# An fp32 mLSTM/attention backbone: activation table loaded during the first transfers, two sums placed later, and key casts regrouped ahead of a layer norm

## The chip, the cores and the metric

The kernel runs on one core of a Trainium2 chip. The metric is the device time of one execution in microseconds (us). The kernel before took 1350.44 us (median of 3 runs, 1350.17 to 1350.73).

## The reference

A backbone of two layers (`DEPTH = 2`) over 256 latent tokens and 256 context tokens of width 1024. Layer 0 mixes tokens with a bidirectional chunkwise mLSTM, layer 1 with multi-head latent attention with a low-rank key/value path; behind each mixer stands a gated convolutional FFN. Each sub-layer reads a modulated input and ends in a layer norm:

```python
# per sub-layer, shift/scale/gate from SiLU(c) @ w_ada + b
h = x * (1 + scale) + shift
x = layer_norm(ALPHA * x + gate * sublayer(h))

# latent attention, layer 1 (cut): kv is compressed, normed, and expanded per head
ckv = rms_norm(h @ w_dkv[..., :256]);  kr = rope(h @ w_dkv[..., 256:])
k_nope = ckv @ w_uk      # 8 heads x 128
v      = ckv @ w_uv      # 8 heads x 128
```

The context stream goes through the same weights with its own modulation and reads only context; the latent stream reads both.

## The kernel before

**Numbers.** Every fp32 operand is split in two parts: a rounded high part (`hi`, a cast on ScalarE, ACT) and the remainder (`lo`, a subtraction on VectorE, DVE). A product is three matmuls on TensorE (PE): hi·hi, hi·lo, lo·hi. `mm3` issues them at L427, L430 and L431, so these three lines hold most matmul rows of the profile, and the names in a row (`y<-w,fz`, `kn<-ckT,wu`, `dkv<-w,hl`) tell which product it is. For activations, `split` issues the cast (L441) and the subtraction (L442).

**Weights** come in banks through a class `Stream`. `_split` casts the high part of a bank on ACT (L344), `low` subtracts its low part on DVE (L367). Low parts of the second pair of `dkv` banks (the layer-1 compression) are kept back and issued by `release`. `pump` runs a stream ahead. `behind(i, others)` fixes that an instruction is queued after others of its own engine; it adds no wait between engines.

**Start.** `start_up` writes the first 20 us out by hand for PE, DVE and ACT: the DMA order in `LOADS`, the instruction order in `STEPS`. `WARM` idle matmuls (L651, product of zeros) come first. Then, by the step letters: `Q` SiLU of the conditioning vector on ACT (L656, `cond`); `a0`/`b0` the two halves of the first 128-wide modulation product (L506, `adar<-adaw,cond`); `I3` three idle matmuls (L667); `C0` copies the product out (ACT); `T0`/`O0` transpose it and make columns; `e0` modulates the first input tile; `w0`, `y0` cast the first weights; `P00`.. are the up-projection matmuls (L714). Every DMA of this stretch is queued on SyncE (SP) at L636.

**Between the layers.** `w_fout0` computes the FFN-out of layer 0 by a Strassen-like scheme: seven products are accumulated in PSUM banks and combined with each other by DVE in the steps of a generator (`sums`); at L1735 the banks of the last product `p7` get the partial sums `u2` added, two instructions of 512 columns. In the same stretch DVE makes the low parts of the weight banks `y21`, `y22` and of `fz`, which PE reads next. 

Then come two layer norms: of the context (a step list `mid(0, ...)`) and of the latent tokens (`mid(1, ...)`), each two row tiles. `z_norm` handles a row tile with `mv` and `rs` (statistics), the first 512 columns on DVE (L1812) and the other 512 on ACT (L1814). `ln_T` transposes the result (16 PE transposes, L1278), applies the norm's scale and shift on ACT (L1284) and DVE (L1285), and splits it into `hc` or `hl`, the input of `dkv`. In its context form `ln_T` calls `release` at its steps 2 and 4. The latent norm is not run as one block: `tick` advances it by a step at points of `build`'s tail, among `mla_kv` (RMS norm and transposes of the compressed kv, `ckr`, `ckT`), `ukn` (keys of eight heads, two heads of 256 columns to a PSUM bank) and `uv` (values). ACT, DVE and PE run their queues strictly in program order.

Of the kernel before, what the change touches and what calls it, by code (L numbers as in the profile page):

```python
# [10 lines left out]
AF = mybir.ActivationFunctionType  # L11
ALU = mybir.AluOpType
# [15 lines left out]
H1 = 8  # L28
# [24 lines left out]

NUP = 5
GATES = 11
WARM = 10
LOADS = (
    "a00 c a01 w0 x0 a10 a11 w1 x1 a20 a21 w2 x2 a30 a31 w3 x3 a40 a41 w4 x4 a50 a51 w5 x5 a60 a61 w6 x6 "
    "a70 a71 x7 w7 s u0 g0").split()
STEPS = (  # L60
# [3 lines left out]
    "A7 C7 K7 V53 T7 O7 V60 E7 k7 V61 H7 V62 V63 V70 V71 V72 V73 U0 V24 V34 V44 V54 V64 V74 M0").split()  # L64
# [81 lines left out]
def _pack(i):  # L146
# [8 lines left out]
    uqr = np.ascontiguousarray(uq[:, :, DN:]).reshape(384, H1 * DR)  # L155
    qn_blocks = np.concatenate([_stat(uqn, h, 0, 3) for h in range(H1)], axis=1)
    kn_blocks = np.concatenate([_stat(ukn, h, 0, 2) for h in range(H1)], axis=1)
    dkv_s = (0, 3, 6)
    for key, (n, cols) in ids.items():
# [97 lines left out]
class Stream:  # L257
# [107 lines left out]
    def low(self, j, src, h, l):  # L365
        n = src.shape[1]
        i = self.k.nc.vector.tensor_sub(l[:, :n], src, h[:, :n])  # L367
        self.k.behind(i, self.behind)
        self.made = i
        self.raw.pop(j)  # L370
        while self._room():
            self._load()
        return i
# [24 lines left out]
class K:  # L398
# [203 lines left out]
    def start_up(self):  # L602

        nc, st = self.nc, self.st
# [9 lines left out]
        for step in LOADS:  # L614
            op, n = step[0], [int(x) for x in step[1:]]
            if op == "a":
                t = raw[step] = self.uf("adaw")
                src = self.a["ada0"][2 * n[0] + n[1]]
            elif op == "x":
                t = raw[step] = self.s2("xT")  # L620
                src = self.a["tokT"][n[0]]
            elif op == "w":
                t = raw[step] = self.pool.tile([128, CW], F32, tag=tag[n[0]][0], name="raw0", bufs=tag[n[0]][1])
                c = slice(0, nw if n[0] < 2 else 512)
                t, src = t[:, c], self.a["up0"][n[0]][:, c]
            elif op == "u":
                t = raw[step] = self.pool.tile([128, CW], F32, tag="raw", name="up4", bufs=NRAW)
                t, src = t[:, :768], self.a["up4"]
            elif op == "c":
                t, src = self.sm0, self.a["sm0"]  # L630
            elif op == "g":
                t = self.gw = self.pool.tile([128, 16, 32], F32, tag="s2", name="gw", bufs=NS)
                src = self.a["gw"]
            else:
                t, src = self.sm, self.a["sm"]
            i = nc.sync.dma_start(t, src)  # L636
# [5 lines left out]
        w = {k: (t[:, 0], t[:, 1]) for k, t in zip((3, 4, 5), w3)}  # L642
        w[0] = [self.pool.tile([128, CW], F32R, tag="acc", name="w0", bufs=2) for _ in range(2)]

        e = mybir.EngineType
        idle = self.ps("idle")
        rows, adas, hT = {}, {}, {}
        ps, made = {}, [0] * NUP
        with self.tc.manual_schedule(engines={e.PE, e.DVE, e.Activation}):
            for _ in range(WARM):  # L650
                nc.tensor.matmul(idle, self.zero[:, 0:128], self.zero, start=True, stop=True)  # L651
            for step in STEPS:
                op, n = step[0], [int(x) for x in step[1:]]
                g = n[0]
# [25 lines left out]
                elif op == "H":  # L680
                    h = hT[g] = self.u("hT")
                    self.split(h[:, 0, :], h[:, 1, :], self.xT[g])
                elif op == "e":
                    h = hT[g] = self.u("hT")
# [8 lines left out]
                elif op in "WwvyzKkU":  # L693
                    if op == "U":
                        g = "u"
# [4 lines left out]
                    hi, lo, src = w[g][0][:, c], w[g][1][:, c], raw["w%s" % g][:, c]  # L700
# [6 lines left out]
                else:  # L707
                    k, m = n
# [606 lines left out]
    def aout_fin(self, o1, pl, xr, gate, fi, h1u, att):  # L1315
# [21 lines left out]
        st.later = []  # L1337
        st.pump(fi + 4)
        low, st.later = st.later, None
        st.behind = lastw  # L1340
        st.pump(fi + 5)
# [313 lines left out]
    def w_fout0(self, x1d, mid):  # L1655


        nc, st, A = self.nc, self.st, self.fa
# [32 lines left out]
        def pair():  # L1691
            return [self.ps("y") for _ in range(2)]

        lo, hi = slice(0, 512), slice(512, 1024)
        p6, p1, p7, p5 = [pair() for _ in range(4)]
        n = 0
        u2 = []
        for i in range(6):
            for name, ps, x in (("yt2", p6, "S2"), ("y11", p1, "1"), ("yt3", p7, "S3"), ("yt1", p5, "S1")):
                w = st.use((name, 0, i))  # L1700
                if (name, i) == ("yt3", 5):
                    for b in range(2):
                        u = self.s2("u1")
# [16 lines left out]
                if n >= 16 and n % 2 == 0:  # L1720
                    if n == 16:
                        z = []
# [4 lines left out]
        stats = [self.tiny(12, "st").rearrange("p (a b) -> p a b", b=6) for _ in range(4)]  # L1727
        vv = []

        def sums():  # L1730
            for b in range(2):
                nc.vector.tensor_tensor(u2[b], p6[b], u2[b], op=ALU.add)
            yield
            for b in range(2):
                nc.vector.tensor_tensor(p7[b], p7[b], u2[b], op=ALU.add)  # L1735
            yield
            for b in range(2):
                v = self.s2("v")
                nc.scalar.copy(v, p7[b])
                nc.vector.tensor_tensor(v, p5[b], v, op=ALU.subtract)  # L1740
                nc.vector.tensor_tensor(p5[b], p5[b], u2[b], op=ALU.subtract)
                vv.append(v)
                yield
# [10 lines left out]
        def last():  # L1754
            for b in range(2):
                add(1, hi, vv, (b,))
                yield

        self.bg.append(sums())
        for i in range(6):  # L1760
            w = st.use(("y21", 0, i))
# [36 lines left out]
        self.fa = self.fd = None  # L1798
        self.bg = [mid(1, z[2:4], stats[2:4], lambda: add(1, lo, p7))]

    def z_norm(self, zs, stats):

        nc = self.nc
        for z, st in zip(zs, stats):
            mv = self.tiny(2, "mv")
            nc.vector.bn_aggr(mv, st)
            rs = self.tiny(1, "rs")
            root = nc.scalar.activation(rs, mv[:, 1:2], AF.Sqrt, bias=self.keps, scale=1.0)
            nc.vector.reciprocal(rs, rs)
            nm = self.tiny(1, "nm")  # L1810
            nc.vector.scalar_tensor_tensor(nm, mv[:, 0:1], -1.0, rs, op0=ALU.mult, op1=ALU.mult)
            rows = nc.vector.tensor_scalar(z[:, 0:512], z[:, 0:512], mv[:, 0:1], rs, op0=ALU.subtract, op1=ALU.mult)  # L1812
            self.normed = rows, root
            nc.scalar.activation(z[:, 512:1024], z[:, 512:1024], AF.Identity, bias=nm, scale=rs)  # L1814
            yield


# [64 lines left out]
                nc.scalar.copy(self.krT[:, 0, cs], p)  # L1882
                nc.vector.tensor_sub(self.krT[0:64, 1, cs], p[0:64], self.krT[0:64, 0, cs])

    def ukn(self, g, heads=range(H1)):

        cs = slice(g * 256, (g + 1) * 256)
        for h in heads:
            w = self.wk[h // 4]
            if h % 2 == 0:  # L1890
                ps = self.ps("kn")
            hs = slice((h % 2) * 256, (h % 2 + 1) * 256)
            for k in range(2):
                c = slice((h % 4) * 256 + k * 128, (h % 4) * 256 + (k + 1) * 128)
                self.mm3(ps[:, hs], (w[0][:, c], w[1][:, c]), (self.ckT[k][:, 0, cs], self.ckT[k][:, 1, cs]),
                         k == 0, k == 1)
            if h % 2:
                for j in range(2):
                    u = self.kn[h - 1 + j]
                    self.split(u[:, 0, cs], u[:, 1, cs], ps[:, j * 256:(j + 1) * 256])  # L1900

    def uv(self, ts):
        for t in ts:
# [213 lines left out]
def build(tc, off, a, out):  # L2117
    es = ExitStack()
    with es:
        k = K(tc, es, off, a)  # L2120
        nc = k.nc
# [72 lines left out]
        pre = k.ffn_pre(0, h0f)  # L2194
# [14 lines left out]
        def half(us):  # L2209
            return lambda i: tuple(us[i // 2][:, n, (i % 2) * 256:(i % 2 + 1) * 256] for n in range(2))  # L2210
        hc, hl = half(hcu), half(hlu)

        def mid(g, zs, stats, first=None):
            if g is None:
                st.limit = kv0 + PA
                k.rope_load()
                k.mla_ctx(hc)
                return
            return norm1(g, zs, stats, first)

        def norm1(g, zs, stats, first):
            A, B = k.ln_mod_cols(1, 1, 0, 1 - g)
            if first is not None:
                first()
                hlu.extend([k.u("hl") for _ in range(4)])
            yield from k.z_norm(zs, stats)
            yield from k.ln_T(zs, A, B, hl if g else hc, g == 1, False, {} if g else {2: st.release, 4: st.release})
            if g:
                k.late.append(k.ln_x(1, zs, [x2d[0], x2d[1]], False))
        k.w_fout0(x1d, mid)  # L2230
        hc = hcu = None
        k.tick(1)
        st.pump(kv0 + PB)
        k.tick(1)
        st.pump(kv0 + PC)
        k.mla_kv()
        k.ukn(0)
        k.uv((0,))
        k.tick(4)
        k.uv((1,))  # L2240
# [3 lines left out]
        hl = hlu = None  # L2244
# [10 lines left out]
        pre = k.aout_fin(o1, pl, xr, gate, fi, h1u, att)  # L2255
# [35 lines left out]
```

## Time and profile before

| what | value |
|---|---|
| device time, median of 3 (lowest, highest) | 1350.44 us (1350.17, 1350.73) |
| device time of the profiled execution | 1350.76 us |
| its span, first to last instruction | 1349.0 us |
| mean granted TensorE clock | 0.999 |
| busy share of the span: PE, DVE, ACT, POOL | 99%, 78%, 53%, 11% |
| DMA over the span | 304 MB moved, mean 225 GB/s |

The 1.76 us between device time and span lie outside of what the trace shows. A timeline row reads: start in us, duration in us, engine, line, operation, output<-inputs, tile (partitions x columns), count, and in brackets the idle time before it with what ended it. On PE the matmuls are pipelined and overlap: a row of 128x512 shows a duration of 0.39 us, while the next one starts 0.23 us later. What a stream of matmuls costs is therefore read from start to start. A row with "SPq" is the issue of a DMA in SP's queue, not its transfer.

### The profile page before, as it was taken

How to read it: one execution, taken by the hardware profiler on the slowest of the kernel's cores; microseconds unless marked ns; L12 is line 12 of the kernel's file. 1: busy time of each engine (PE TensorE's matmuls, PEld its weight loads, DVE VectorE, ACT ScalarE, POOL GpSimd, SP SyncE). 2: the span in 40 equal slices, each digit the busy share in tenths (PEclk: the TensorE clock that was granted, in tenths of full speed). 3: DMA queues.
4: the chain of work that ended last, by engine and by line, in shares of the span. 5: the costliest groups of instructions: out<-in, count | busy, mean ns of one | idle time of the engine just before them, and what ended most of it. 6: DMA issues, size and time to landing. Idle time of an engine off the chain costs nothing.

```text
span 1349.0 us, 18773 instructions
## 1 busy us (share of the span) xinstructions
PE 1338.7 (99%) x6662; PEld 1120.8 (83%) x6662; DVE 1057.8 (78%) x1749; ACT 711.0 (53%) x1251; POOL 142.2 (11%) x236
## 2 busy tenths in 40 slices
PE   9999999999999999999999999999999999999997
PEld 5777888888888888888898888888888998988886
DVE  4798657678688696897979977758899789898873
ACT  4765444445744546364643334333566768676660
POOL 0212000011101011030002011111000002000100
PEclk9999999999999999999999999999999999999999
DMA  9988848889687374785628989967875537366850
GB/s 359 323 279 286 280 156 251 234 289 305 217 279 233 96 258 132 247 293 218 213 93 262 321 258 282 283 183 190 291 228 187 158 98 219 129 212 188 262 189 32
DMA packets 99885, 304.02 MB, mean 225 GB/s; under 512 B 12312, under 2 KB 25112, under 8 KB 99712
## 3 DMA queue, kind: packets, MB, share of 16 engines
q1 hardware_dynamic: 62992, 218.65, 48.7%
q0 software_dynamic: 26000, 66.75, 17.8%
q10 hardware_dynamic: 10800, 17.44, 3.6%
q8 instruction: 52, 0.85, 0.3%
q14 instruction: 41, 0.34, 0.1%
HBM read 272.21 MB, written 42.12 MB: 233 GB/s over the span
## 4 chain that ended last, share of the span: by engine, by line
PE 99%; DVE 0%; DMA 0%; ACT 0%; issue 0%; DVEq 0%; SPq 0%; ACTq 0%
PE fin L1483 8%; PE y L430 6%; PE y L427 6%; PE y L431 6%; PE fin L427 6%; PE tok L427 6%; PE fin L430 6%; PE fin L431 6%; PE tok L430 6%; PE tok L431 6%; PE qk L427 4%; PE qk L431 4%; PE qk L430 4%; PE up L714 2%; PE up L427 1%; PE up L430 1%
## 5 line engine op out<-in xcount | busy, mean ns | idle before, releaser
L344 ACT CAST w<-raw 128x1024 fp32r<-128x1024 f32 (+2 forms) x286 | 296.5, 1038 | 293.8 <-PE tok L431 83.3
L367 DVE TENSOR_TENSOR w<-raw,w 128x1024 fp32r<-128x1024 f32 (+2 forms) x286 | 343.0, 1202 | 138.1 <-ACT w L344 135.6
L541 DVE SCALAR_TENSOR_TENSOR junk<-ar,bc 128x1024 f32<-128x1024 f32 x128 | 155.9, 1218 | 5.1 <-ACT bc L583 2.4
L430 PE MATMUL fin<-h,w 128*128 128x512 f32 (+1 forms) x376 | 141.2, 376 | 0.0
L431 PE MATMUL fin<-h,w 128*128 128x512 f32 (+1 forms) x376 | 140.9, 375 | 0.0
L427 PE MATMUL fin<-h,w 128*128 128x512 f32 (+1 forms) x376 | 140.8, 376 | 0.1
L1483 PE MATMUL fin<-h,w 128*128 128x512 f32 (+1 forms) x636 | 111.1, 337 | 0.0
L1483 PEld LDWEIGHTS fin<-h,w 128*128 128x128 f32 x636 | 97.6, 190 | 13.2
L427 PE MATMUL qk<-xc,w 128*128 128x512 f32 x256 | 100.6, 393 | 0.0
L431 PE MATMUL qk<-xc,w 128*128 128x512 f32 x256 | 99.9, 390 | 0.0
L430 PE MATMUL qk<-xc,w 128*128 128x512 f32 x256 | 99.8, 390 | 0.0
L430 PEld LDWEIGHTS fin<-h,w 128*128 128x128 f32 x376 | 70.8, 188 | 12.9 <-DVE h L1311 0.2
L431 PEld LDWEIGHTS fin<-h,w 128*128 128x128 f32 x376 | 70.8, 188 | 12.9
L427 PEld LDWEIGHTS fin<-h,w 128*128 128x128 f32 x376 | 70.6, 188 | 13.1 <-ACT h L1310 0.3
L431 PEld LDWEIGHTS qk<-xc,w 128*128 128x128 f32 x256 | 48.1, 188 | 9.9
L427 PEld LDWEIGHTS qk<-xc,w 128*128 128x128 f32 x256 | 48.1, 188 | 9.7
L430 PEld LDWEIGHTS qk<-xc,w 128*128 128x128 f32 x256 | 48.1, 188 | 9.6
L427 PE MATMUL tok<-w,hT 128*128 128x512 f32 x128 | 49.9, 390 | 0.0
L430 PE MATMUL tok<-w,hT 128*128 128x512 f32 x128 | 49.8, 389 | 0.0
L431 PE MATMUL tok<-w,hT 128*128 128x512 f32 x128 | 49.8, 389 | 0.0
L731 ACT ACTIVATE fg<-fg 128x512 f32<-128x512 f32 (+1 forms) x44 | 23.1, 525 | 47.2 <-DVE fg L729 41.1
L367 DVE TENSOR_TENSOR wu<-raw,wu 128x1024 fp32r<-128x1024 f32 (+1 forms) x37 | 43.7, 1200 | 3.1 <-ACT wu L344 2.9
(484 smaller groups left out, 3128.5 us busy)
## 6 DMA issues: line engine op xcount, KB each, us to landing
raw<-in_ws SPq DMA_DIRECT2D x282, 512.0 KB, 4.5
ar<-in_adaT SPq DMA_DIRECT2D x80, 512.0 KB, 4.8
t4d<-in_ws POOLq DMA_DIRECT2D x20, 512.0 KB, 9.3
adaw<-in_ada SPq DMA_DIRECT2D x16, 512.0 KB, 7.9
zr<-fd ACTq DMA_DIRECT2D x33, 128.0 KB, 4.3
xmd<-xr POOLq DMA_DIRECT2D x16, 256.0 KB, 4.6
xcd<-cv POOLq DMA_DIRECT2D x16, 256.0 KB, 5.0
xs<-xmd POOLq DMA_DIRECT2D x16, 256.0 KB, 5.5
```

The source lines that it names most:

```text
L344: self.cast = k.nc.scalar.copy(h[:, :cols], src)
L367: i = self.k.nc.vector.tensor_sub(l[:, :n], src, h[:, :n])
L427: q = mm(out, w[0], x[0], start=start, stop=False, skip_group_check=on)
L430: mm(out, w[0], x[1], start=False, stop=False, skip_group_check=on)
L431: mm(out, w[1], x[0], start=False, stop=stop, skip_group_check=on)
L541: nc.vector.scalar_tensor_tensor(o, w, 1.0, self.bc[j], op0=ALU.mult, op1=ALU.mult, accum_out=col[:, k, j:j + 1])
L714: nc.tensor.matmul(ps[m], wk[i][:, c], hT[k][:, j], start=made[m] == 0, stop=made[m] == 23)
L731: nc.scalar.activation(tmp[:, :n], tmp[:, :n], AF.Silu)
L1483: self.nc.tensor.matmul(ps[:, 0:256] if x else ps, w[x][:, k * 128:(k + 1) * 128], h[:, 0:256] if x else h, start=i == 0 and not k0, stop= ...
```

## The change

Four edits.

1. `WARM` goes from 10 to 8 and `I3` to `I2`; ahead of the start-up list stands a SiLU of a one-column constant (`keps`, set by a DVE memset), whose result `pre` nobody reads.
2. Both additions of `u2` to `p7` are queued on DVE behind the low part of the weight bank `("y21", 0, 1)`.
3. Context norm: the first `release` is called before `ln_T` and no more at its step 2.
4. Latent norm and keys. In `ukn` both casts of a PSUM bank are issued first and both subtractions behind them (before: cast, subtraction, cast, subtraction). For the heads 0 to 3 the casts are placed directly and the four subtractions held back; the ACT half of the first normed row tile (`zrest`) is issued behind these casts, the next `tick` of the norm behind that, and the held subtractions are queued behind the norm's DVE half of the second tile. The second `tick` is no more between the two pumps.

```diff
-WARM = 10
+WARM = 8
-    "Q0 a0 I3 b0 C0 w0 I1 T0 O0 y0 e0 I5 P00 P01 ...
+    "Q0 a0 I2 b0 C0 w0 I1 T0 O0 y0 e0 I5 P00 P01 ...
 # Stream.low
         self.made = i
+        if self.order[j][0] == ("y21", 0, 1):
+            self.second = i
 # start_up
+        self.tc.keep_in_program_order(nc.scalar.activation(self.tiny(1, "pre"), self.keps, AF.Silu))
 # w_fout0, sums
             for b in range(2):
-                nc.vector.tensor_tensor(p7[b], p7[b], u2[b], op=ALU.add)
+                self.behind(nc.vector.tensor_tensor(p7[b], p7[b], u2[b], op=ALU.add), [st.second])
 # z_norm(self, zs, stats, held=False)
-            nc.scalar.activation(z[:, 512:1024], z[:, 512:1024], AF.Identity, bias=nm, scale=rs)
+            rest = lambda z=z, nm=nm, rs=rs: nc.scalar.activation(z[:, 512:1024], z[:, 512:1024], AF.Identity,
+                                                                  bias=nm, scale=rs)
+            if held:
+                self.zrest, held = rest, False
+            else:
+                rest()
 # ukn(self, g, heads=range(H1), held=None)
             if h % 2:
+                lows = []
                 for j in range(2):
-                    u = self.kn[h - 1 + j]
-                    self.split(u[:, 0, cs], u[:, 1, cs], ps[:, j * 256:(j + 1) * 256])
+                    hi, lo, src = self.kn[h - 1 + j][:, 0, cs], self.kn[h - 1 + j][:, 1, cs], ps[:, j * 256:(j + 1) * 256]
+                    i = self.nc.scalar.copy(hi, src)
+                    if held is not None:
+                        self.tc.keep_in_program_order(i)
+                    lows.append(lambda lo=lo, src=src, hi=hi: self.nc.vector.tensor_sub(lo, src, hi))
+                if held is not None:
+                    held += lows
+                else:
+                    for low in lows:
+                        low()
 # build, mid
-            yield from k.z_norm(zs, stats)
-            yield from k.ln_T(zs, A, B, hl if g else hc, g == 1, False, {} if g else {2: st.release, 4: st.release})
+            yield from k.z_norm(zs, stats, g == 1)
+            if not g:
+                st.release()
+            yield from k.ln_T(zs, A, B, hl if g else hc, g == 1, False, {} if g else {4: st.release})
 # build, tail
         k.tick(1)
         st.pump(kv0 + PB)
-        k.tick(1)
         st.pump(kv0 + PC)
         k.mla_kv()
-        k.ukn(0)
+        held = []
+        k.ukn(0, range(4), held)
+        k.tc.keep_in_program_order(k.zrest())
+        k.tick(1)
+        for low in held:
+            k.behind(low(), k.normed)
+        k.ukn(0, range(4, H1))
         k.uv((0,))
```

In the changed kernel line numbers are higher by 3 at the start (L656 is L659, L506 is L508) and near the sums (L1735 is L1738); the key casts are L1909, their subtractions L1912.

On PE the program begins with the idle matmuls and the first modulation product. Before:

```order
L651 MATMUL idle<-zero 128x512 x10
L506 MATMUL adar<-adaw,cond 32x256 x4
L667 MATMUL idle<-zero 128x512 x3
L506 MATMUL adar<-adaw,cond 32x256 x4
L667 MATMUL idle<-zero 128x512
```

and now:

```order
L654 MATMUL idle<-zero 128x512 x8
L508 MATMUL adar<-adaw,cond 32x256 x4
L670 MATMUL idle<-zero 128x512 x2
L508 MATMUL adar<-adaw,cond 32x256 x4
L670 MATMUL idle<-zero 128x512
```

Three idle matmuls are gone, two ahead of `a0` and one ahead of `b0`; the rows behind are those of before.

On DVE in the sums of `w_fout0` (`y` are the PSUM banks of `p7`, `u1` the partial sums, `w` the weight bank's low part). Before, with buffer numbers:

```order
L1735 TENSOR_TENSOR y_7993<-y_7993,u1_8457 128x512
L1678 TENSOR_TENSOR fz_8470<-zr_8427,fz_8470 128x512
L367 TENSOR_TENSOR w_8475<-raw_8229,w_8475 128x1024
L1735 TENSOR_TENSOR y_7994<-y_7994,u1_8459 128x512
L1678 TENSOR_TENSOR fz_8489<-zr_8446,fz_8489 128x512
L367 TENSOR_TENSOR w_8496<-raw_8255,w_8496 128x1024
```

and now:

```order
L1681 TENSOR_TENSOR fz_8469<-zr_8426,fz_8469 128x512
L367 TENSOR_TENSOR w_8474<-raw_8228,w_8474 128x1024
L1738 TENSOR_TENSOR y_7992<-y_7992,u1_8456 128x512
L1681 TENSOR_TENSOR fz_8488<-zr_8445,fz_8488 128x512
L1738 TENSOR_TENSOR y_7993<-y_7993,u1_8458 128x512
L367 TENSOR_TENSOR w_8495<-raw_8254,w_8495 128x1024
```

The first addition moved from ahead of the first low part to behind it; the second stays between the two low parts.

On ACT at the latent norm (`z` is a normed row tile's second half, `kn` the high part of a head's keys). Before:

```order
L1814 ACTIVATE z_8433<-z_8433,nm_9027,rs_9024 128x512
L1808 ACTIVATE rs_9045<-mv_9043,keps_73 128x1
L441 CAST kn_9064<-kn_9072 128x256
L441 CAST kn_9065<-kn_9072 128x256
L1814 ACTIVATE z_8473<-z_8473,nm_9048,rs_9045 128x512
L441 CAST kn_9066<-kn_9089 128x256
```

and now:

```order
L1909 CAST kn_9053<-kn_9061 128x256
L1909 CAST kn_9054<-kn_9061 128x256
L1909 CAST kn_9055<-kn_9076 128x256
L1909 CAST kn_9056<-kn_9076 128x256
L1817 ACTIVATE z_8432<-z_8432,nm_9026,rs_9023 128x512
L1811 ACTIVATE rs_9094<-mv_9092,keps_73 128x1
L1909 CAST kn_9057<-kn_9105 128x256
L1909 CAST kn_9058<-kn_9105 128x256
L1817 ACTIVATE z_8472<-z_8472,nm_9097,rs_9094 128x512
```

Four key casts now stand ahead of the first row tile's ACT half, and two more ahead of the second row tile's. On DVE all eight key subtractions stand in one run behind the second row tile's half (L1815).

More of the change, by code (lines that the diff above doesn't have):

```diff
@@ L1799, in w_fout0, with z_norm @@
         self.bg = [mid(1, z[2:4], stats[2:4], lambda: add(1, lo, p7))]
-    def z_norm(self, zs, stats):
+    def z_norm(self, zs, stats, held=False):
         nc = self.nc
@@ L1883, in dkv_T, with ukn @@
                 nc.vector.tensor_sub(self.krT[0:64, 1, cs], p[0:64], self.krT[0:64, 0, cs])
-    def ukn(self, g, heads=range(H1)):
+    def ukn(self, g, heads=range(H1), held=None):
         cs = slice(g * 256, (g + 1) * 256)
```

2 rows, old and new, of the table STEPS are left out of this document.

## Prediction

> **What bounds the kernel now.** I read the chain that ended last first, then what PE waits for over the whole span:
>
> ```profile
> PE 99%; DVE 0%; DMA 0%; ACT 0%; issue 0%; DVEq 0%; SPq 0%; ACTq 0%
> PE idle L651 <- DVE adav L494: 1.5, 1, 1.5
> ```
>
> PE is the chain, and its longest listed wait (us, times, longest) is the 1.5 us before its first instruction; the only two others, 0.25 and 0.19, stand in brackets in the rows of edit 1. No other engine's work sets the end, so an edit is worth what it takes out of PE's time from start to start, in its own stretch. Stalls of a few tenths don't show as waits: a late input stretches a matmul's row. So I went to the timeline at each edited place and compared starts.
>
> **Edit 1, the start.** The timeline of PE, of ACT, and of SP's queue:
>
> ```profile
> 1.49 4.64 PE L651 MATMUL idle<-zero 128*128 128x512 f32 x10 [1.49 <-DVE adav L494]
> 5.07 1.06 PE L651 MATMUL idle<-zero 128*128 128x512 f32 x2
> 6.32 1.05 PE L506 MATMUL adar<-adaw,cond 128*32 128x256 f32 x8 [0.19 <-ACT cond L656]
> 7.30 0.98 PE L667 MATMUL idle<-zero 128*128 128x512 f32 x3
> 8.21 0.64 PE L506 MATMUL adar<-adaw,cond 128*32 128x256 f32 x8
> 11.20 1.61 PE L714 MATMUL up<-hT,w 128*128 128x512 f32 x6 [0.25 <-DVE hT L689]
> 16.48 1.07 PE L506 MATMUL adar<-adaw,cond 128*32 128x256 f32 x16
> ...
> 4.76 1.28 ACT L656 ACT_TABLE_LOAD   x1 [4.76 <-DMA sm<-in_sm]
> 6.06 0.22 ACT L656 ACTIVATE cond<-sm 128x16 f32<-128x16 f32 x1
> ...
> 7.59 0.33 SPq L636 DMA_DIRECT2D adaw<-in_ada  x1
> 9.04 0.33 SPq L636 DMA_DIRECT2D xT<-in_tokT  x1
> 14.38 1.62 SPq L636 DMA_DIRECT2D adaw<-in_ada  x2
> ```
>
> The table load sits behind the DMA of `sm`, though it needs nothing of it; `a0` (6.32) follows the end of `cond` (6.28) by 0.04. The dummy SiLU reads a constant that a DVE memset writes ahead of PE's first row, so the load now runs from about 1.5 to 2.8, where ACT has nothing else. `cond` then runs from 4.76 to 4.98, and `a0` could start at 5.02; PE takes it behind its eighth idle matmul, at 5.07, where the row of the last two begins. That is 1.25 before 6.32. `a0` takes 0.98 to the next row, until 6.05. The first idle matmuls go at (5.07 - 1.49)/8 = 0.45 each, the later ones at (8.21 - 7.30)/3 = 0.30: two take 0.6 to 0.9, and `b0` could start between 6.65 and 6.95.
>
> But `b0` reads the other half of the weights, `a01`. I read landings in SP's queue: a ninth issue goes out only when the one eight places earlier has landed. The issue at 7.59 is that of `a21`, eight places behind `a01` in `LOADS`; so `a01` landed just before 7.59. `b0` starts at 7.6 and not at 8.21: a gain of **0.6**, with some 0.65 of new idle time on PE ahead of it. What follows is a chain on `b0` (`C0`, `T0`, `O0`, `e0`), and `P00` moves from 11.20 to 10.6 unless another transfer is late. The first tile `x0` had landed by 9.04 (the issue of `x2`), over a microsecond before that. The later modulation weights have the least room at `a21`, read off the second issue of the row at 14.38: it starts at 14.38 + 1.62 - 0.33 = 15.67, and its product starts at 16.48, so 0.6 earlier leaves 0.2. Bounds: 0.23 (one full-speed 128x512 step, rows of edit 2) if only the idle matmul ahead of `b0` is saved; 1.5 (8.21 - 6.7) if `a01` lands earlier than in this execution.
>
> **Edit 2, the sums.** The timeline of DVE and of PE:
>
> ```profile
> 984.02 0.69 DVE L1735 TENSOR_TENSOR y<-y,u 128x512 f32<-128x512 f32 x1
> 985.22 1.22 DVE L367 TENSOR_TENSOR w<-raw,w 128x1024 fp32r<-128x1024 f32 x1
> 987.55 1.22 DVE L367 TENSOR_TENSOR w<-raw,w 128x1024 fp32r<-128x1024 f32 x1
> ...
> 985.61 0.39 PE L431 MATMUL y<-w,fz 128*128 128x512 f32 x1
> 985.83 0.61 PE L427 MATMUL y<-w,fz 128*128 128x512 f32 x2
> 986.83 0.40 PE L431 MATMUL y<-w,fz 128*128 128x512 f32 x1
> 988.89 0.39 PE L427 MATMUL y<-w,fz 128*128 128x512 f32 x1
> ```
>
> A step is 0.23 (985.61 to 985.83). From 985.83 to 986.83 PE makes three (two of L427, and an L430 between the rows) in 1.00 instead of 0.68: it waits for the low part that DVE ends at 986.44. Without the first sum ahead of it (its row says 0.69, and such instructions overlap by 0.08), this low part ends 0.6 earlier, at 985.84, which is ahead of its use. Gain **0.32**. The second low part has the same work ahead of it on DVE as before, both sums among it, and stays at 987.55 to 988.77; from the order of the products it is read around 988.9, now 988.6. So up to 0.32 can be paid again there: bounds 0 and 0.32. I take the upper end, since between 986.83 and 988.89 PE runs nine steps of 0.23 without a stretch, so its stall in these rows is at the first bank alone. The sums' own reader on ACT comes microseconds later.
>
> **Edit 3, context norm.** DVE, ACT and PE:
>
> ```profile
> 1022.81 0.54 DVE L1285 TENSOR_SCALAR zm<-zT,lnA,lnB 128x256 f32<-128x256 f32 x1 [1.18 <-PE zT L1278]
> 1025.67 1.15 DVE L367 TENSOR_TENSOR w<-raw,w 128x960 fp32r<-128x960 f32 x1
> ...
> 1021.01 1.69 ACT L344 CAST w<-raw 128x960 fp32r<-128x960 f32 x2
> ...
> 1026.43 0.46 PE L427 MATMUL dkv<-w,hc 128*128 128x320 f32 x2
> 1027.13 0.30 PE L431 MATMUL dkv<-w,hc 128*128 128x320 f32 x1
> ```
>
> A 128x320 step is 320/512 of 0.23, or 0.145. The three from 1026.43 to 1027.13 (an L430 between the rows) take 0.70 instead of 0.44, waiting for the low part that ends at 1026.82. Gain **0.26**. Now the low part goes ahead of `ln_T`, where DVE stood idle for 1.18. Its cast is the first or second of the pair from 1021.01; if the second, it is there at about 1022.0 to 1022.7, the low part ends at 1023.2 to 1023.8, and the first DVE `zm` moves from 1022.81 by 0.4 to 1.0. PE reads that tile as its second, over 1.5 later. Bounds: the 0.26 gained, or 0.1 lost if `zm` comes late.
>
> **Edit 4, keys and latent norm.** PE, DVE, ACT, and a row of the waits in this stretch:
>
> ```profile
> 1039.29 0.28 PE L430 MATMUL kn<-ckT,wu 128*128 128x256 f32 x1
> 1039.67 0.28 PE L427 MATMUL kn<-ckT,wu 128*128 128x256 f32 x1
> 1051.91 0.39 PE L431 MATMUL v<-wu,ckT 128*128 128x512 f32 x1
> 1052.54 0.31 PE L430 MATMUL dkv<-w,hl 128*128 128x320 f32 x1
> ...
> 1038.19 1.20 DVE L367 TENSOR_TENSOR wu<-raw,wu 128x1024 fp32r<-128x1024 f32 x1
> 1045.71 0.53 DVE L1812 TENSOR_SCALAR z<-z,mv,rs 128x512 f32<-128x512 f32 x1
> 1047.99 0.76 DVE L442 TENSOR_TENSOR kn<-kn 128x256 fp32r<-128x256 f32 x2 [0.44 <-ACT kn L441]
> ...
> 1043.70 0.82 ACT L1814 ACTIVATE z<-z,nm,rs 128x512 f32<-128x512 f32 x1 [2.31 <-DVE nm L1811]
> 1046.02 0.82 ACT L1814 ACTIVATE z<-z,nm,rs 128x512 f32<-128x512 f32 x1
> 1048.21 1.02 ACT L1284 ACTIVATE zm<-zT,lnB,lnA 128x256 f32<-128x256 f32 x2
> 1050.80 1.13 ACT L441 CAST v<-v 128x512 fp32r<-128x512 f32 x2
> 1051.76 2.62 ACT L1291 CAST hl<-zm 128x256 fp32r<-128x256 f32 x8
> ...
> ACT kn L441 <- DVE kn L442: 1.3, 2, 0.8
> ```
>
> Two places. First, two 128x256 steps take 0.38 (1039.29 to 1039.67) instead of 0.23: the keys wait for a bank's low part that ends at 1039.39. One norm instruction of 0.6 no longer stands ahead of it: **0.14**. Second, a 128x512 and a 128x320 step take 0.63 (1051.91 to 1052.54) instead of 0.38: PE waits for the first `hl`, whose cast begins at 1051.76. It is late because ACT's casts and DVE's subtractions of the keys took turns: ACT waited 1.3 in two waits. Now ACT casts four keys in the 2.31 that it stood idle before 1043.70, so its norm halves stay near 1043.6 and 1046.1; behind the second stand two key casts (0.65 with their overlap), the two casts of `v` (1.0), two `zm` (1.0) and then `hl`, which so begins at about 1046.9 + 2.65 = 1049.6. PE wants it two microseconds later: **0.25**.
>
> What is late next: DVE's eight key subtractions now stand in one run behind the second row tile's DVE half, which I put at 1046.3 (before: 1045.71 + 0.53 = 1046.24). At 0.34 each (0.76 for two, with their overlap) they end at 1049.0. Behind them are DVE's `zm` for the second `hl`, then its cast: 1049.0, two subtractions of 0.6, two `zm` of 0.5 and a cast of 0.4 give at the latest 1052.5 with the waits between, and PE wants that at 1053.0. Margin 0.45. The subtractions also hold the keys' PSUM banks: the third is wanted by PE at about 1049.0, and its subtractions end at 1048.3. Margin 0.7. Bounds: 0.39 gained, or 1.0 lost where DVE slips by more than these margins (a slip of one weight bank's low part, 1.2).
>
> **The sum.** 0.6 + 0.32 + 0.26 + 0.14 + 0.25 = 1.57. The profiled execution took 1350.76 (span 1349.0, and 1.76 around it): it would take 1349.2. It lies 0.32 above the median of the runs, so on the median's footing 1350.44 - 1.57 = **1348.9**. A measurement of this kernel tells about 0.2% (2.7 us) from no change, and the forecast is inside that.
>
> **Rivals.**
>
> *The load doesn't move* (0.08). If it still ended at 6.04, edit 1 would save only the 0.23: 1350.44 - 0.23 - 0.97 = 1349.2. For it: only the order moves the load, nothing in the trace shows one without its DMA. Against: its own activation reads no DMA.
>
> *PE stays slow for longer* (0.16). The rows show PE slow at first: 0.45 per idle matmul up to 5.07, but 0.30 from 7.30. It doubled its pace near 7, after 5.5 us of nearly unbroken work; now there are three idle matmuls less and a gap of 0.65 that begins at 6.95. If the doubling slips past `b0` and its successors, edit 1 is eaten: 1350.44 - 0.97 = 1349.5 (0.10). If it slips to about 14, the six `up` matmuls from 10.6, three more and the sixteen short ones ahead of 14 run at half pace: nine steps of 0.23 and half the row of 1.07 are added, 2.6, less the 0.95 that the idle matmuls and `b0` already lost to it: +1.65, so 1350.44 + 1.65 - 0.97 = **1351.2**, slower than before (0.06). The point that decides is whether PE has worked long enough by 6.95. [...]
>
> *DVE slips in edit 4* (0.12): the 0.39 is lost and 0.8 is paid at the third bank and the second `hl`: 1350.44 - 1.18 + 0.8 = 1350.1. For it: four casts stand ahead of the norm on ACT. Against: ACT stood idle there.
>
> *The transfer isn't the limit* (0.06): with `a01` before 7, edit 1 gives 1.5 and the time is 1348.0.
>
> **Numbers.** The forecast has 0.58. The range, 1347.8 to 1350.6, runs from the last rival, less 0.2 (the runs before lie up to 0.29 from their median), to the DVE slip with edit 2's or 3's gain lost as well. Only several of the bounds together pass 2.7 either way: faster 0.05, slower 0.05, within 0.90.
>
> **What would show it.** Right: the table load at 1.5, `cond` at 4.76, `a0` at 5.07, `b0` at 7.6, `P00` at 10.6; no stretched row at the four places named (986, 1026.5, 1039.4, 1052, less the shift up to there). Wrong: `b0` before 7.4 or after 8; 0.45 per 128x512 step behind `b0`; a stretched row at about 988.6; the second row tile's DVE half 0.7 later against PE; a stretched `v` or `dkv` row behind the transposes.

## The result

The changed kernel took 1348.49 us (median of 22 runs, 1348.10 to 1349.57), the kernel before, run beside it as often, 1350.41 us (1350.11 to 1350.79). The ratio is 0.9986 with a 95% interval of 0.998 to 0.9993, which leaves out 1: 1.9 us faster, inside the range and 0.4 below the forecast. The profiled execution is the slowest of the 22: 1349.57 us with a span of 1347.8, only 1.2 us below the profiled one of before. Two more profiled executions of the same kernel stand in the experiments.

What PE waits for in the changed kernel, over the whole span:

```profile
PE idle L654 <- DVE adav L496: 1.5, 1, 1.5
PE adar L508 <- DMA adaw<-in_ada: 0.7, 1, 0.7
PE up L717 <- DVE hT L692: 0.3, 1, 0.3
PE y L432 <- DVE w L367: 0.2, 1, 0.2
```

The second row is the landing that the prediction named; the fourth is new and was not foreseen. The timeline of the start, PE and then ACT:

```profile
1.50 3.78 PE L654 MATMUL idle<-zero 128*128 128x512 f32 x8 [1.50 <-DVE adav L496]
5.21 1.08 PE L508 MATMUL adar<-adaw,cond 128*32 128x256 f32 x8
6.22 0.97 PE L670 MATMUL idle<-zero 128*128 128x512 f32 x2
7.88 0.64 PE L508 MATMUL adar<-adaw,cond 128*32 128x256 f32 x8 [0.69 <-DMA adaw<-in_ada]
10.86 1.63 PE L717 MATMUL up<-hT,w 128*128 128x512 f32 x6 [0.26 <-DVE hT L692]
...
0.74 1.28 ACT L647 ACT_TABLE_LOAD   x1 [0.74 <-PEq L2305]
4.75 0.22 ACT L659 ACTIVATE cond<-sm 128x16 f32<-128x16 f32 x1 [2.51 <-DMA sm<-in_sm]
```

`cond` runs where it was put (4.75), `a0` at 5.21, and `b0` waits for `a01` until 7.88, 0.33 before its old start; `P00` follows with 0.34. In every profile in which `b0` waits for `a01`, it starts 0.02 to 0.03 behind the issue of `a21` (here 7.85, the second of a row of SP's queue), so the way in which the prediction read landings held.

At the sums and behind them, PE, ACT and DVE:

```profile
985.50 0.61 PE L429 MATMUL y<-w,fz 128*128 128x512 f32 x2
985.95 0.39 PE L432 MATMUL y<-w,fz 128*128 128x512 f32 x1
997.78 0.39 PE L429 MATMUL y<-w,fz 128*128 128x512 f32 x1
998.36 0.50 PE L432 MATMUL y<-w,fz 128*128 128x512 f32 x1 [0.20 <-DVE w L367]
998.70 0.40 PE L433 MATMUL y<-w,fz 128*128 128x512 f32 x1
...
994.19 0.41 ACT L1679 CAST fz<-zr 128x256 fp32r<-128x256 f32 x1 [1.59 <-DMA zr<-fd]
994.62 1.28 ACT L1776 ACT_TABLE_LOAD   x1
996.02 3.01 ACT L344 CAST w<-raw 128x1024 fp32r<-128x1024 f32 x3
...
997.08 2.36 DVE L367 TENSOR_TENSOR w<-raw,w 128x1024 fp32r<-128x1024 f32 x2 [1.15 <-ACT w L344]
```

The stretch at 986 is gone: three steps from 985.50 would end at 986.18, and the row at 985.95 is a plain 0.39. But from 997.78 two steps take 0.92 instead of 0.45: 0.47 is paid. ACT's casts of the next weight bank stand behind a table load, and that behind a cast of `zr` (loaded by DMA, cast into the high part of `fz`) that waits for its transfer until 994.19. In the kernel before that cast began even later:

```profile
994.34 0.41 ACT L1676 CAST fz<-zr 128x256 fp32r<-128x256 f32 x1 [0.84 <-DMA zr<-fd]
```

No row is stretched there, since the product that now starts at 997.78 started at 998.41. So the late transfer alone did not stretch the row; with PE 0.63 earlier it did.

At the context norm DVE makes the second low part before `zm`, and at the latent norm the subtractions run in one row:

```profile
1021.87 1.16 DVE L367 TENSOR_TENSOR w<-raw,w 128x960 fp32r<-128x960 f32 x1 [0.39 <-ACT w L344]
1022.95 0.54 DVE L1288 TENSOR_SCALAR zm<-zT,lnA,lnB 128x256 f32<-128x256 f32 x1
1045.18 0.54 DVE L1815 TENSOR_SCALAR z<-z,mv,rs 128x512 f32<-128x512 f32 x1
1045.63 2.74 DVE L1912 TENSOR_TENSOR kn<-kn 128x256 fp32r<-128x256 f32 x8
...
1048.47 0.70 ACT L1294 CAST hl<-zm 128x256 fp32r<-128x256 f32 x2
...
1046.70 1.91 PE L1281 MATMUL zT<-ident,z 128*128 128x128 f32 x16
1048.37 0.47 PE L429 MATMUL v<-wu,ckT 128*128 128x512 f32 x1
1051.21 0.30 PE L429 MATMUL dkv<-w,hl 128*128 128x320 f32 x1
```

No `dkv` row is stretched, and the eight subtractions take 2.74 as forecast. One thing was not forecast: `v` follows the start of the 16 transposes by 1.67. In the kernel before, PE's rows and the waits of this stretch read

```profile
1047.35 1.91 PE L1278 MATMUL zT<-ident,z 128*128 128x128 f32 x16
1049.28 0.50 PE L427 MATMUL v<-wu,ckT 128*128 128x512 f32 x1
PEld v L427 <- ACT zm L1284: 0.3, 1, 0.3
```

so it was 1.93 there, with a wait for ACT's `zm`. `v` uses nothing that `zm` makes, so it must have waited for a PSUM bank that `zm` reads. In the changed kernel `v` starts (1048.37) before ACT's pair of `zm` ends (1047.56 + 1.02 = 1048.58), so it no longer waits for the second of them; how the edit brings that about, no run shows.

### The profile page after: what moved, and what is told of

It reads as the page before. It is cut to its first block, busy times and chain, and to the rows that moved or that the text cites. A ratio compares the mean times of both kernels' runs of the same rounds, so it can differ in the third digit from the quotient of the medians.

```text
span 1347.8 us, 18768 instructions
## 1 busy us (share of the span) xinstructions
PE 1336.9 (99%) x6659; PEld 1120.1 (83%) x6659; DVE 1058.3 (79%) x1749; ACT 710.6 (53%) x1252; POOL 141.7 (11%) x236
## 4 chain that ended last, share of the span: by engine, by line
PE 97%; DMA 1%; DVE 1%; ACT 0%; issue 0%; ACTq 0%; SPq 0%; DVEq 0%
PE fin L1486 8%; PE fin L432 6%; PE fin L429 6%; PE tok L429 6%; PE tok L432 6%; PE fin L433 6%; PE tok L433 6%; PE y L432 6%; PE y L433 6%; PE y L429 6%; PE qk L429 4%; PE qk L433 4%; PE qk L432 4%; PE up L717 2%; PE up L429 1%; PE up L432 1%
```

## The experiments

To place the time, I compared the same instruction's start in two traces: the first `zT` of the context norm, the first `kn`, the first `dq` (the product behind the latent `dkv`), and so on. In what follows "moved by" means that difference against the profiled execution of before. A span that moved by the same amount ahead of an edit and behind it gained nothing there.

**Each edit alone.** Edit 1 alone:

```diff
-WARM = 10
+WARM = 8
-    "Q0 a0 I3 b0 ...
+    "Q0 a0 I2 b0 ...
+        self.tc.keep_in_program_order(nc.scalar.activation(self.tiny(1, "pre"), self.keps, AF.Silu))
```

> The kernel before with edit 1 alone (dummy SiLU, 8 and 2 idle matmuls). Theory 1: b0 begins when a01 has landed, 0.3 to 0.6 earlier than before, and PE is that much earlier up to the FFN-out; around 998 us a weight bank's low part, whose casts stand behind a DMA wait and a table load on ACT, takes back what goes beyond about 0.2: 1350.1 to 1350.2. Theory 2 (what PE gains at the start it keeps to the end, and the start gains more in most executions than in the profiled one of the changed kernel): 1349.4 to 1349.8.

Measured: 1349.93 us (before on the same chip 1350.44; the ratio's interval, 0.9988 to 1.0005, holds 1). In its profile `b0` began at 7.37, behind the idle matmuls, and not behind the transfer, which had landed by 6.42 (the issue of `a21`); `P00` had moved by -0.76, and the end by -0.80. What the start gains stays to the end: theory 1's pay-back at 998 did not occur here.

The dummy SiLU alone is only the last line of that diff:

> The kernel before with the dummy SiLU alone, 10 and 3 idle matmuls as before. Theory 1 (the idle matmuls ahead are in the way): a0 at 6.1 behind the tenth idle matmul instead of 6.32, b0 at 8.0 instead of 8.21: 0.2 less, 1350.2. Theory 2 (the table load is the whole of edit 1): as a_only.

Measured: 1350.09 (before 1350.44). Its profile is of the slowest of its eleven executions (1350.70). There the load was done early, `a0` began at 6.06, and yet `b0` began at 8.20, unmoved:

```profile
6.06 1.08 PE L506 MATMUL adar<-adaw,cond 128*32 128x256 f32 x8
7.07 1.20 PE L668 MATMUL idle<-zero 128*128 128x512 f32 x3
8.20 0.64 PE L506 MATMUL adar<-adaw,cond 128*32 128x256 f32 x8
```

The three idle matmuls took 1.13 from start to start, against 0.91 in the profile of before: PE's pace doubled later, only within them. So the load alone saves what the idle matmuls ahead leave of it, and in this execution that went to a later doubling.

Edit 2 alone is the `behind(..., [st.second])` of the diff:

> The kernel before with edit 2 alone (both sums behind the low part). Theory 1: the stretched rows at 986 go (0.32 gained), and a stretched row comes at about 998.4 that pays 0.1 to 0.3 of it back: 1350.2 to 1350.3. Theory 2 (the gain stays): 1350.1. If the pay-back is larger than the gain: 1350.4 or above.

Measured: 1350.04 (before 1350.44). Its profile moved by +0.04 ahead of the sums and by -0.32 at the first `zT`: 0.36 gained, and no stretched row at 998. The pay-back is not a consequence of edit 2 as such: here the last `zr` cast began at 993.65.

Edit 4 alone:

> The kernel before with edit 4 alone (keys and latent norm). Theory 1: besides the 0.14 and 0.25 of the prediction the six ckT transposes run without a break (0.1) and the third bank of v no longer waits for ACT's zm (0.28): 0.77 in all, 1349.6. Theory 2 (only what the prediction named): 0.39, 1350.0.

Measured: 1349.80 (before 1350.44). From the transposes on, its profile goes from -0.38 to -0.94 at `dq`: 0.55 (the `v` bank and `hl`). But the row of 1039.45 is stretched as before: from -0.40 at the first `kn` to -0.40 at the first `v`. The 0.14 that the prediction ascribed to this edit is not its. On DVE the low part that these keys read still stands behind the norm's statistics (1037.79 behind 1037.19), as in the kernel before.

Edit 3 alone:

```diff
             yield from k.z_norm(zs, stats)
-            yield from k.ln_T(..., {} if g else {2: st.release, 4: st.release})
+            if not g:
+                st.release()
+            yield from k.ln_T(..., {} if g else {4: st.release})
```

> The kernel before with edit 3 alone (the kept low part released ahead of ln_T). Theory 1: the stretched rows at 1026.5 go, 0.26 less: 1350.15. Theory 2 (the pushed-back zm makes a later dkv row wait): 1350.4 or more, with a stretched dkv row at about 1025.

Measured: 1349.73 (before 1350.36). In the profile -0.43 at the first `dkv` of the context becomes -0.81 at the first `kn` and -0.95 at the first `v`: 0.52 for an edit priced at 0.26. The six `ckT` transposes stand in one row, where the profile of before has five, two stretched products, and one:

```profile
1033.82 0.82 PE L1872 MATMUL ckT<-ident,ckr 128*128 128x128 f32 x6
```

That is 0.11, and the 0.14 at the keys is here too. In this trace DVE has the two `ckr` copies behind each other ahead of a product of the gate, which before stood between them; the order of DVE's queue differs there as well once `release` has moved. The low part that the keys read now stands ahead of the norm's statistics (1037.61):

```profile
1036.47 1.21 DVE L367 TENSOR_TENSOR wu<-raw,wu 128x1024 fp32r<-128x1024 f32 x1
```

It ends at 1037.68, before the first key product (1037.89); in the kernel before it ended at 1039.39, in the middle of the keys.

The intervals of all these single-edit ratios hold 1, so no edit alone is measured as faster; the parts are read from rows of one profiled execution each. The medians of the four edits lie 0.51, 0.40, 0.64 and 0.63 (edits 1, 2, 4, 3) below before, 2.18 in sum, against 1.92 for the whole.

**The spread between executions.** The changed kernel, unaltered, again:

> The changed kernel once more, for a second profiled execution. Theory 1: what differs between its executions is when a01 lands (6.5 to 7.9 in the profiles so far) and when PE's pace doubles at the start, and whether the last zr transfer (issued at about 988.6) lands over 5 us later: with an earlier landing the stretched row at 998 is gone, and the median of 1348.5 is the usual case. Theory 2 (the row at 998 is stretched in every execution): the row stands again, 0.3 to 0.5 long.

> The changed kernel a third time, as the mate of the next two on the same chip: 1348.4 to 1348.9, with b0 waiting for a01 or standing right behind the two idle matmuls.

Measured: 1348.82 (1347.88 to 1350.29) and 1348.40 (1347.88 to 1349.03). The starts of the two profiled executions, PE:

```profile
5.20 0.64 PE L508 MATMUL adar<-adaw,cond 128*32 128x256 f32 x8
5.77 0.73 PE L670 MATMUL idle<-zero 128*128 128x512 f32 x2
7.62 0.64 PE L508 MATMUL adar<-adaw,cond 128*32 128x256 f32 x8 [1.11 <-DMA adaw<-in_ada]
```
```profile
5.21 1.06 PE L508 MATMUL adar<-adaw,cond 128*32 128x256 f32 x8
6.19 0.73 PE L670 MATMUL idle<-zero 128*128 128x512 f32 x2
6.86 0.64 PE L508 MATMUL adar<-adaw,cond 128*32 128x256 f32 x8
```

With identical code `a0` took 0.57 in one and 0.98 in the other: PE's pace had doubled before 5.2, and only then about 6.2. `a01` landed at 7.6 in one and before 6.9 in the other. `P00` moved by -0.60 and -1.36, by 0.76 more; the device times of the two executions, 1348.84 and 1348.02, differ by 0.82. Neither has the stretched row at 998: the last `zr` had landed at 993.15 and 992.66 and not at 994.19. So the row of the first profile takes a late transfer besides the earlier PE, and does not come in every execution; theory 2 of that run falls.

In the first of these two profiles, a weaker form of the prediction's lower bound for edit 2 shows, PE and DVE:

```profile
987.98 0.61 PE L429 MATMUL y<-w,fz 128*128 128x512 f32 x2
988.46 0.50 PE L432 MATMUL y<-w,fz 128*128 128x512 f32 x1
988.79 0.39 PE L433 MATMUL y<-w,fz 128*128 128x512 f32 x1
...
987.18 1.22 DVE L367 TENSOR_TENSOR w<-raw,w 128x1024 fp32r<-128x1024 f32 x1
```

The second bank's low part ends at 988.40, and three steps take 0.81 instead of 0.68: 0.13 of the 0.32 is paid again. In the third execution the same three steps take 0.69, and the move up to the first `zT` grows by 0.28, against 0.20 here.

The start that edit 1 doesn't touch varies as well. `P00` began at 11.20, 11.23, 10.82 and 10.75 in the profiles of before and of edits 2, 4 and 3 alone, which is why the last two stand at about -0.4 ahead of their edits. With edit 1's start (edit 1 alone, three executions of the changed kernel, and two variants of it below that alter only later stretches) it began at 10.44, 10.86, 10.60, 9.84, 10.54 and 9.98. The means are 11.00 and 10.38, 0.62 apart, and the two sets overlap by a little.

**Less work ahead of the doubling.** Without the two idle matmuls between `a0` and `b0`:

```diff
-    "Q0 a0 I2 b0 ...
+    "Q0 a0 b0 ...
```

> The changed kernel without the two idle matmuls between a0 and b0. Theory 1: b0 begins when a01 has landed and not before 6.3, so 0 to 0.9 earlier than in the changed kernel, and 0.2 to 0.4 less in the median: 1348.1 to 1348.3. Theory 2 (PE's pace doubles only after work without a gap, which is cut here): the doubling comes behind b0 or later in a part of the executions, 0.5 to 1.7 more: 1349 or above, with a wider spread.

Measured: 1349.44 (1348.14 to 1349.94), against 1348.82 of the unaltered kernel on the same chip. In its profiled execution `b0` began at 7.59 behind the transfer and ran at full pace (0.57 to the next row); that execution, at 1348.99, doesn't show why the median is 0.6 higher. The ranges overlap (unaltered 1347.88 to 1350.29), and the spread is not wider, so the time leans to theory 2 and shows no cause.

With `a01` issued ahead of `sm`:

```diff
-    "a00 c a01 w0 x0 ...
+    "a00 a01 c w0 x0 ...
```

> The changed kernel with a01 issued ahead of sm in SP's queue. Theory 1 (a01's landing sets b0): a01 lands up to 0.45 earlier and sm 0.45 later, so a0 begins at about 5.5 and b0 at 7.1 to 7.5 instead of 7.6: 0.1 to 0.4 less. Theory 2 (the transfers share the bandwidth and the queue order matters little, or a0 with its idle matmuls becomes the bound): as the changed kernel or up to 0.3 more.

Measured: 1349.98, and the eleven times fall into two groups, five from 1348.43 to 1348.76 and six from 1349.98 to 1350.42. The profile is of the second group (1350.34):

```profile
6.31 1.08 PE L508 MATMUL adar<-adaw,cond 128*32 128x256 f32 x8 [1.03 <-ACT cond L659]
7.32 1.22 PE L670 MATMUL idle<-zero 128*128 128x512 f32 x2
8.47 1.08 PE L508 MATMUL adar<-adaw,cond 128*32 128x256 f32 x8
9.49 0.80 PE L670 MATMUL idle<-zero 128*128 128x512 f32 x1
12.11 1.17 PE L717 MATMUL up<-hT,w 128*128 128x512 f32 x4 [0.27 <-DVE hT L692]
```

`sm` landed 1.3 later and not 0.45 (ACT's `cond` at 6.04), and PE had a gap of 1.03 ahead of `a0`. `a01` had landed by 5.74 (the issue of `a20`, eight places behind it), so `b0` no longer waited for it. `a0` and `b0` both took 1.01 to 1.02, so PE stayed at half pace until past 9.5, and `P00` moved by +0.91. That is the prediction's second rival, seen in a kernel next to this one. Whether the five faster executions lacked the gap, or doubled earlier behind it, no profile shows. Behind the same eight idle matmuls PE's pace had doubled by 4.96 in one trace (the last variant below, whose `a0` took 0.57) and did so only past 9.5 in this one. What sets the moment no run shows; that it is decided by enough work up to 6.95 was the author's estimate from one trace (5.5 us of work ahead of a doubling near 7).

**Taking the new exposures away.** The square root's table load ahead of ACT's last `fz` cast instead of behind it:

```diff
+                if not parts and not got:
+                    pin(nc.scalar.activation(self.tiny(1, "pre"), self.keps, AF.Sqrt))
                 cut[:] = [nc.scalar.copy(u[:, 0, :n], r[:, :n])]
-        self.behind(nc.scalar.activation(self.tiny(1, "pre"), self.keps, AF.Sqrt), cut)
```

> The changed kernel with one more edit: the square root's table load of the FFN-out stands ahead of ACT's last fz cast, which waits for the zr transfer, and no more behind it. Theory 1: the casts behind come up to 1.4 earlier wherever zr lands late, no stretched row at 998 in any execution; 0.1 to 0.45 less than the changed kernel in the median (1348.1 to 1348.4) and a smaller spread upward. Theory 2 (the low parts there are early enough in the usual execution): as the changed kernel, 1348.5.

Measured: 1348.57 (1348.06 to 1348.90), against 1348.82 (1347.88 to 1350.29) on the same chip. ACT in its profile:

```profile
992.17 1.28 ACT L1680 ACT_TABLE_LOAD   x1
993.58 0.39 ACT L1681 CAST fz<-zr 128x256 fp32r<-128x256 f32 x1
993.87 1.04 ACT L344 CAST w<-raw 128x1024 fp32r<-128x1024 f32 x1
996.46 1.05 ACT L344 CAST w<-raw 128x1024 fp32r<-128x1024 f32 x1 [1.54 <-PE y L433]
```

The load now lies in the wait, the first cast follows `fz` at once, and ACT then waits 1.54 for PE: the slack is there. The second bank's low part is late here too: the three steps from 987.89 take 0.86 instead of 0.68. The median's 0.25 is less than these runs can tell.

With the sums behind the second bank's low part as well:

```diff
-        if self.order[j][0] == ("y21", 0, 1):
+        if self.order[j][0] == ("y21", 0, 2):
```

> The changed kernel with the table load ahead of the last fz cast, and with the two sums queued behind the second bank's low part, ('y21', 0, 2), and no more behind the first's. Theory 1 (the second low part comes too late by 0.13 in the last profile, since both sums stand ahead of it): no stretched row at 986 and none at 988.5, 0.1 to 0.2 less than the table edit alone, 1348.3 to 1348.4. Theory 2 (the stretch passes on to the third bank): a stretched row at about 990.7, nothing gained.

Measured: 1348.40 (1347.78 to 1348.66), ratio to before 0.9984 (0.9975 to 0.9993); the unaltered changed kernel on the same chip took 1348.40 as well. No row of its profile is stretched by 0.1 or more between 980 and 1002, and the move from the start to the first `zT` is 0.36, against 0.20 and 0.28 in the second and third execution of the unaltered kernel. It takes the last stretched rows away, its upper end is the lowest of all kernels, and it is not measurably faster.

## Why the prediction was right, and where its steps were off

- **Edit 1 (0.6).** The mechanism held: `cond` at 4.75, `b0` set by `a01`, a gap of 0.7 to 1.1 ahead of it in two of the three profiles. Single executions differ: over three the start gained 0.34, 0.60 and 1.36 against one profiled execution of before. On the mean of the profiles it is 0.62, so the size held as well, but from one landing that was by luck near the middle. The step that was too narrow was to read one landing (7.59) and one doubling of PE's pace (about 7) as fixed; among the profiles with edit 1's start `a01` landed between 6.42 and 7.85. The two idle matmuls ahead of `b0`, put at 0.6 to 0.9, took 1.15 at half pace in the profile of edit 1 alone (6.22 to 7.37), and there they set `b0`.
- **Edit 2 (0.32).** 0.36 alone, 0.20 and 0.28 in the whole (second and third execution): the step that took the upper end because PE ran "without a stretch" up to 988.89 was wrong, as the second bank's low part was already just in time and PE came earlier. In the first profiled execution 0.47 was paid at 998 besides, which was no term of the sum.
- **Edit 3 (0.26).** 0.52. The stall went as costed and `zm` cost nothing (1022.95, 0.14 later, where 0.4 to 1.0 was expected). The other half came from rows that the edit's own stretch did not hold: 0.11 at `ckT` and 0.14 at the keys. The 0.14 was in the sum, but under edit 4 and for a reason that edit 4 alone did not bear out.
- **Edit 4 (0.39).** 0.55, with a wrong part: the 0.14 is edit 3's, and the 0.27 at the third `v` bank was not seen. The 0.25 at `hl` and the lateness of the subtractions came as costed; the cast of the first `hl` began 2.7 before its use.
- **The sum.** Of the second execution: 0.60 + 0.20 + 0.52 + 0.55 = 1.87, against 1.92 between its time, 1348.84, and that of the profiled execution of before. The forecast's 1.57 was short by the side effects of edits 3 and 4 less the loss in edit 2.
- **The signs and the figures.** Two of the signs of being wrong did come, in one execution each: `b0` before 7.4 (6.86, third) and a stretched row at about 988.6 (988.46, second). Two figures do not add up as written: 1350.44 + 1.65 - 0.97 is 1351.1, not 1351.2, and the upper end of the range comes to 1350.4 (1350.1 + 0.32), or 1350.6 only with another 0.2 for the spread.
- **The rivals.** The load moved, to 0.74 and not 1.5: it did not wait for the memset of `keps` either, which DVE begins at 1.39. The slip of DVE did not come: the second row tile's DVE half ended at 1045.72, 0.52 earlier than before, in a stretch that had moved by 0.65. The late doubling did not show in a profile of the changed kernel; it did with one more gap ahead of it. The early `a01` showed once in the changed kernel, with a time of 1348.02 where the rival said 1348.0; the start gained 1.36 and not 1.5, and the other edits more than the rival counted, so the match is partly luck.

## What to carry to other kernels

When work is pulled out of a wait at the start of a program, the next transfer may set its gain, as it did here in five profiles (`b0` 0.02 to 0.03 behind the issue that shows the landing of `a01`), and over the profiles with edit 1's start that landing varied from 6.42 to 7.85: read it from several executions, of the kernel before as well, not from one. Price a moved instruction also where the order of a queue may change behind it; running each edit alone showed half of edit 3's gain (0.25 of 0.52) in rows it does not touch. When PE comes earlier, look for the inputs that were just in time before (0.47 paid at 998 in one execution, 0.13 at 988 in another).

## What was not expected of the hardware

PE's pace doubled between before 5.0 us (the last variant, whose `a0` began at 4.96) and after 9.5 us (`a01` ahead of `sm`) in executions that began with the same eight idle matmuls; `a0`'s eight rows took 0.57 or about 1.0. The transfer of 512 KB that `b0` reads had landed between 6.42 and 7.85 with its issue at 1.65 to 1.67. In the kernel with `a01` ahead of `sm`, the profile with a gap of 1.03 ahead of `a0` belongs to a group of times about 1.5 us higher, more than the gap itself; the other group has no profile.
